# A float32 transformer block: the up projection of ten column quads as Strassen block products, and the down projection taken quad by quad with its sums added in DRAM

## Chip, cores and metric

The kernel runs on one core of one Trainium2 chip. Its time is device microseconds of one launch; the figure compared is the median of several launches. Engines are named as in the profile: PE (TensorE, matrix products), PEld (the weight loads of PE, which run beside its products), DVE (VectorE), ACT (ScalarE), POOL (GpSimd), SP (SyncE, which here only issues transfers).

## The reference

One block of a hybrid backbone: a token mixer of two scanned head groups and, behind it, a gated MLP. The change lies in the MLP, which works on 512 latent tokens (a grid of 8 rows by 64 columns), 2048 channels and 5504 hidden channels:

```python
h2 = rmsnorm(x, g_norm2) * (1 + sc2) + sh2
x = x + gt2 * conv_ffn(h2, rows, GRID_W, w_up, conv_w, conv_b, w_down)

def conv_ffn(h, rows, cols, w_up, conv_w, conv_b, w_down):
    u = jnp.einsum('btd,df->btf', h, w_up)
    u_gate, u_val = jnp.split(u, 2, axis=-1)
    g = lax.conv_general_dilated(u_gate.reshape(b, rows, cols, D_FF), conv_w[:, :, None, :],
                                 window_strides=(1, 1), padding='SAME',
                                 dimension_numbers=('NHWC', 'HWIO', 'NHWC'),
                                 feature_group_count=D_FF)
    g = g.reshape(b, t, D_FF) + conv_b
    return jnp.einsum('btf,fd->btd', jax.nn.silu(g) * u_val, w_down)
```

The convolution is depthwise, 3x3 and centred. A last RMS norm over channels gives the output. sh2, sc2 and gt2 are three of six slices of a modulation vector, one row times a 2048 x 12288 matrix. All inputs are float32.

## The kernel before

**Numbers and layout.** Activations lie channels by tokens: a tile is 128 channels (partitions) by 512 tokens. PE takes a reduced float32, so every operand is kept as a pair, the rounded value (h or hi) and the remainder (l or lo): `split` (L88 to L90) has ScalarE cast the value (L89) and VectorE subtract it (L90). `mm3` (L104) multiplies two such pairs with three matmuls, hi by hi, hi by lo and lo by hi, and all matmuls stand in the profile as L95. Likewise `mul` is L83 and `add` L86 wherever they are called.

**Weights.** They come in chunks of 512 KB, two row blocks of 128 by 512 columns. `load_split` (L162) asks SP for the chunk into one of the raw buffers of `wraw` (four), and splits it into one of two hi and one of two lo buffers (`whi`, `wlo`). `unit` (L197) is one product of 2048 channels by 512 output columns for all tokens: eight chunks, each with 4 column blocks x 2 row blocks x 3 matmuls of 512 columns, 192 matmuls into four PSUM accumulators. Pool psA has six of the eight PSUM banks and psB two.

**Order.** The code of `block_kernel` runs once, to lay out the program. A scheduler puts the instructions into each engine's queue in the order of the code, with those under `tc.high_priority()` moved ahead; where `pinned` is set, PE's order is exactly that of the code. A queue is worked in order, and each instruction waits for its inputs and for the tile that it reuses.

**Modulation as filler.** Four of the six slices of the modulation are summed on VectorE: `mod_chunk` (L259) loads a raw tile of `w_mod` and adds two rows of it, times a scalar, into a running sum (L272, L274). `mod_fillers` lists these pieces, and `load_split` takes some per chunk by a rate (`rate`, `credit`; the lists `UG_FILL` and `UV_FILL` in the MLP). The slice gt2 (region 5) is summed in the first quads of the MLP, since it is wanted only at the first residual.

**Stages in order.** Input projection with the scans woven in; gate projections `ga` (four units); output projection `wo` (four units), which ends with the residual into `x2`, kept in SBUF as 16 tiles, and the token norm. Then h2 (L1057 to L1066): for each of 16 row blocks VectorE scales x2 into `t`, a tile of a pool with two buffers, ScalarE casts it with the shift added, VectorE forms the remainder. Then the MLP by quads of four hidden row blocks (`QUADS`: ten of four and a last one of three):

- `up_gate` (L1092) is one unit on the gate columns. ScalarE copies each accumulator into a padded grid (L1099) and starts the convolution with one tap (L1106); VectorE adds eight taps (L1108), ScalarE applies silu. The first unit, `ug0`, starts while h2 is still being made: with `late` its first chunk takes all hi products of the two first row blocks ahead of those with a remainder (L183 to L189).
- `up_val` (L1113) is one unit on the value columns; VectorE multiplies each accumulator into the gated value, and the product is split into `gh` and `gl`.
- `down_block` (L1128) multiplies the products of a group of quads with 512 output columns of `w_down` and adds the four accumulators to x2 on VectorE, times gt2 (`residual`, L1004). `GROUPS` takes two quads at a time, and the last three together (11 row blocks); the four blocks of a group run between the gate unit and the value unit of the quad behind it.

**Tail.** Behind the last value unit come three blocks of the last group, with the squares for the last norm, then the fourth (`dl`) in two halves of 256 tokens. In the second half's matmuls, at places 10 and 18 of 44, PE takes the first half's norm (`token_rstd`) and VectorE, GpSimd and the output transfers take its scaling (`scaled`, L1170). The second half's own norm, scaling and outputs end the program.

## Time and profile before

| what | value |
|---|---|
| time, median of 3 launches (lowest, highest) | 2572.23 us (2571.21, 2572.74) |
| profiled execution: span on the chip | 2571.5 us |
| HBM read, written | 315.10 MB, 4.19 MB |
| granted PE clock, mean | 0.997 of full |
| busy time of the sixteen transfer engines, q1 (SP) | 36.8% of the span |

The busy line gives busy time per engine, its share of the span, and the number of instructions. The chain is the work that ended last, followed back from the end. In rows of groups, `out<-in` are the names of tiles with their numbers left out; behind the bar stand busy time and mean ns of one, then the idle time ahead of them and what ended it. Rows of a timeline give start, duration, engine, line, operation, tiles, shape and the number of like instructions in a row. Rows of windows give the stretch, its length, the busy time of PE, weight loads, VectorE, ScalarE and GpSimd with their counts, then granted clock, share of the transfer engines, and GB/s.

### The profile page before, as it was taken

The numbers are of one execution on the slowest core, as the hardware profiler recorded it, in microseconds if no ns is written. First come the engines' busy times: TensorE is split into PE (matmuls) and PEld (weight loads), VectorE is DVE, ScalarE is ACT, GpSimd is POOL, SyncE is SP. The second block draws the span as 40 slices with busy tenths as digits, with TensorE's granted clock in tenths as the row PEclk, the third lists the DMA queues.
The fourth block names the chain that finished last, engine by engine and source line by source line (L and its number), as shares of the span: only waits on it lengthen the run. The fifth ranks groups of instructions, "written<-read, shape, count | busy, mean of one in ns | idle before, by whom it ended". The sixth has DMA issues, their size and how long they took to land.

```text
span 2571.5 us, 31635 instructions
## 1 busy us (share of the span) xinstructions
PE 2532.5 (98%) x12944; PEld 2125.0 (83%) x12944; DVE 1399.4 (54%) x2071; ACT 789.2 (31%) x1177; POOL 25.1 (1%) x53
## 2 busy tenths in 40 slices
PE   6999999999999999999999999999999999999998
PEld 4887899888887888888888888888888888888887
DVE  6567755544446676549856335632663365336534
ACT  4225543322223242234323122312331233123332
POOL 0000000000000000000000000000000000000001
PEclk9999999999999999999999999999999999999999
DMA  9741111132335776325733332332232233322333
GB/s 384 265 166 34 34 42 49 59 96 86 130 126 191 250 270 236 129 81 166 259 99 98 98 99 94 95 98 99 99 97 93 97 99 99 99 95 88 101 94 107
DMA packets 96345, 321.35 MB, mean 125 GB/s; under 512 B 10884, under 2 KB 15304, under 8 KB 96200
## 3 DMA queue, kind: packets, MB, share of 16 engines
q1 hardware_dynamic: 95112, 318.29, 36.8%
q8 instruction: 101, 1.65, 0.3%
q10 hardware_dynamic: 1088, 1.05, 0.1%
q14 instruction: 44, 0.36, 0.0%
HBM read 315.10 MB, written 4.19 MB: 124 GB/s over the span
## 4 chain that ended last, share of the span: by engine, by line
PE 95%; DVE 3%; ACT 1%; issue 1%; DMA 0%; SPq 0%; DVEq 0%; ACTq 0%
PE a L95 19%; PE ug L95 18%; PE dn L95 17%; PE uv L95 17%; PE ga L95 7%; PE wo L95 7%; PE po L95 4%; PE ps_m L95 1%; PE sl L95 1%; PE dl L95 1%; DVE cv L1108 1%; PE cst L95 1%; PE s L95 1%; DVE sq_l L86 0%; PE gm L95 0%
## 5 line engine op out<-in xcount | busy, mean ns | idle before, releaser
L95 PE MATMUL uv<-h2h,hi_uv 128*128 128x512 f32 x688 | 267.7, 389 | 0.0
L95 PE MATMUL uv<-h2l,hi_uv 128*128 128x512 f32 x688 | 267.6, 389 | 0.0
L95 PE MATMUL uv<-h2h,lo_uv 128*128 128x512 f32 x688 | 267.6, 389 | 0.0
L95 PE MATMUL ug<-h2h,hi_ug 128*128 128x512 f32 x688 | 267.4, 390 | 0.0
L95 PE MATMUL ug<-h2h,lo_ug 128*128 128x512 f32 x688 | 266.7, 389 | 0.7 <-DVE lo_ug L90 0.7
L95 PE MATMUL ug<-h2l,hi_ug 128*128 128x512 f32 x688 | 266.6, 389 | 0.0
L95 PE MATMUL dn<-gh,hi_d 128*128 128x512 f32 x644 | 250.5, 389 | 0.0
L95 PE MATMUL dn<-gl,hi_d 128*128 128x512 f32 x644 | 250.5, 389 | 0.0
L95 PE MATMUL dn<-gh,lo_d 128*128 128x512 f32 x644 | 250.5, 389 | 0.0
L1108 DVE SCALAR_TENSOR_TENSOR cv<-pad,cwt,cv 128x512 f32<-128x512 f32 x344 | 237.5, 747 | 8.5 <-ACT cv L1106 7.2
L90 DVE TENSOR_TENSOR lo_ug<-raw_ug,hi_ug 128x1024 fp32r<-128x1024 f32 (+1 forms) x88 | 105.5, 1199 | 248.9 <-ACT hi_ug L89 248.9
L90 DVE TENSOR_TENSOR lo_uv<-raw_uv,hi_uv 128x1024 fp32r<-128x1024 f32 (+1 forms) x88 | 105.4, 1198 | 174.8 <-ACT hi_uv L89 174.4
L90 DVE TENSOR_TENSOR lo_d<-raw_d,hi_d 128x1024 fp32r<-128x1024 f32 x82 | 98.7, 1204 | 169.7 <-ACT hi_d L89 168.8
L274 DVE SCALAR_TENSOR_TENSOR sum_m<-raw_m,csil,sum_m 128x512 f32<-128x512 f32 x240 | 179.9, 750 | 19.5 <-DMA raw_m<-in_w_mod 13.9
L89 ACT CAST hi_ug<-raw_ug 128x1024 fp32r<-128x1024 f32 (+1 forms) x88 | 90.9, 1033 | 304.8 <-PE ug L95 220.9
L89 ACT CAST hi_d<-raw_d 128x1024 fp32r<-128x1024 f32 x82 | 85.1, 1037 | 278.7 <-PE dn L95 224.4
L89 ACT CAST hi_uv<-raw_uv 128x1024 fp32r<-128x1024 f32 (+1 forms) x88 | 90.8, 1032 | 257.0 <-PE uv L95 176.7
L95 PEld LDWEIGHTS ug<-h2h,lo_ug 128*128 128x128 f32 x688 | 129.2, 188 | 28.0 <-DVE lo_ug L90 1.3
L95 PEld LDWEIGHTS ug<-h2h,hi_ug 128*128 128x128 f32 x688 | 129.1, 188 | 27.6 <-issue 0.8
L95 PEld LDWEIGHTS uv<-h2h,hi_uv 128*128 128x128 f32 x688 | 129.2, 188 | 26.8
L95 PEld LDWEIGHTS uv<-h2h,lo_uv 128*128 128x128 f32 x688 | 129.2, 188 | 26.7
L95 PEld LDWEIGHTS uv<-h2l,hi_uv 128*128 128x128 f32 x688 | 129.2, 188 | 26.7
(307 smaller groups left out, 4934.0 us busy)
## 6 DMA issues: line engine op xcount, KB each, us to landing
raw_m<-in_w_mod SPq DMA_DIRECT2D x192, 512.0 KB, 5.0
raw_ug<-in_w_up SPq DMA_DIRECT2D x80, 512.0 KB, 3.3
raw_uv<-in_w_up SPq DMA_DIRECT2D x80, 512.0 KB, 3.4
raw_d<-in_w_down SPq DMA_DIRECT2D x79, 512.0 KB, 3.4
raw_h<-in_w_heads SPq DMA_DIRECT2D x64, 512.0 KB, 3.3
raw_ga<-in_w_gates SPq DMA_DIRECT2D x32, 512.0 KB, 4.2
raw_wo<-in_w_out SPq DMA_DIRECT2D x32, 512.0 KB, 3.3
xl<-in_xT SPq DMA_DIRECT2D x16, 256.0 KB, 5.1
```

Source lines behind the costliest of these rows:

```text
L89: S.copy(hi, x)
L90: return V.tensor_tensor(out=lo, in0=x, in1=hi.bitcast(F32), op=ALU.subtract).ins
L95: ins = PE.matmul(*args, **kw)
L274: V.scalar_tensor_tensor(out=parts[0], in0=x, scalar=ck, in1=parts[0], op0=ALU.mult, op1=ALU.add)
L1108: V.scalar_tensor_tensor(out=t3, in0=src, scalar=w, in1=t3, op0=ALU.mult, op1=ALU.add)
```

## The change

**Up projection.** A unit is a product of a 2 x 2 block matrix (per chunk two row blocks of channels; two halves of 256 hidden columns) with another (the two row blocks; two halves of 256 tokens). For the ten quads of four it becomes Strassen's seven products, in the form that shares sums. `load_sums` takes the place of `load_split`: the raw tile has 7 x 256 columns, four quarters from DRAM and three sums on VectorE (`add` three times, one of them over a quarter no longer needed), and the split covers all 1792 columns. The tokens' operands are four halves `bq` (one of them overwritten later by a sum, `token_last`) and three sums `bt`, hi and lo each, made once by `token_sums`. `seven` issues 7 products x 2 column blocks x 3 matmuls of 256 columns for each of eight chunks, into seven PSUM tiles out of a pool of eight banks (`psM`). `four` folds the seven sums into the four quarters of the output through two tiles u and v. In a gate unit `put` writes a quarter into the padded grid; in a value unit it multiplies it into the gated value and, once both token halves are there, splits the products.

**Order of quads.** The quad of three comes first and stays in plain form, and the token sums are made behind its gate unit in the code. h2's first step writes over x2 in place of a tile `t`, after x2 has been stored to DRAM (`x2d`).

**Down projection.** It runs quad by quad between the next quad's gate and value unit. `down_sums` has ScalarE copy each accumulator into one of three staging tiles (`stp`), and GpSimd's queue adds it to DRAM with an accumulating transfer: for the first nine quads to `dacc`, unscaled, for the next to `x2d`, times gt2. `fold`, behind the down stage of the ninth quad (index `FOLD` = 8), reads `dacc` back, scales it, and adds it to `x2d`. At the end x2 is read back into SBUF. The modulation pieces are spread over these down stages at 0.7 a chunk in place of the two lists.

**Tail.** The last group has four row blocks in place of eleven, so the first half's norm and scaling stand at places 4 and 8 of 16. The weights of `w_up` are cut accordingly.

```diff
-QUADS = [4] * 10 + [3]
-GROUPS = [[0, 1], [2, 3], [4, 5], [6, 7], [8, 9, 10]]
+QUADS = [3] + [4] * 10
+NQ = len(QUADS)
+FOLD = NQ - 3
...
+    def fill():
         credit[0] += rate[0]
         while credit[0] >= 1:
             credit[0] -= 1
             if fillers:
                 fillers.pop(0)()
...
+    def load_sums(src, name):
+        x = wts[0].tile([P, 7, HW], F32, name=f"raw_{name}", tag="raw")
+        hi = wts[1].tile([P, 7, HW], F32R, name=f"hi_{name}", tag="hi")
+        lo = wts[2].tile([P, 7, HW], F32R, name=f"lo_{name}", tag="lo")
+        nc.sync.dma_start(x[:, 0:4, :], src.rearrange("p a (b c) -> p (a b) c", c=HW))
+        with tc.high_priority():
+            add(x[:, 4:6, :], x[:, 0:4:3, :], x[:, 1:2, :].to_broadcast([P, 2, HW]))
+            add(x[:, 6, :], x[:, 5, :], x[:, 0, :])
+            add(x[:, 1, :], x[:, 2, :], x[:, 6, :])
+            split(hi, lo, x)
+        fill()
         return hi, lo
...
+    x2d = [dram.tile([P, T], F32, name=f"x2d{k}", tag=f"x{k}") for k in range(KT)]
+    dacc = [dram.tile([P, T], F32, name=f"dacc{k}", tag=f"d{k}") for k in range(KT)]
...
+                nc.gpsimd.dma_start(x2d[4 * n + i], x2[4 * n + i])
...
+    wts[:] = [pool(ctx, "mraw", 3, waits="tile"), pool(ctx, "mhi", 2, waits="tile"), pool(ctx, "mlo", 2, waits="tile")]
+    bp = pool(ctx, "bp", waits="tile")
+    fp = pool(ctx, "fp", waits="tile")
+    stp = pool(ctx, "stp", 3, waits="tile")
+    mod_raw.append(wts[0])
+    rate[0] = 0
...
+    bq = [[operand(j, part, "q", f"bq{part}{j}", (P, 4, HW)) for j in range(KP)] for part in "hl"]
+    bt = [[operand(j, part, "t", f"bt{part}{j}", (P, 3, HW)) for j in range(KP)] for part in "hl"]
+    h2 = [[flat(b[k // 2][:, 2 * (k % 2) : 2 * (k % 2) + 2, :]) for k in range(KT)] for b in bq]
...
-            t = gp.tile([P, T], F32, name=f"h2_{k}", tag="h2")
             sk, bk = modc[4][:, k : k + 1], modc[3][:, k : k + 1]
-            h2[0].append(acttile(k, "h", f"h2h{k}"))
-            h2[1].append(acttile(k, "l", f"h2l{k}"))
-            V.scalar_tensor_tensor(out=t, in0=x2[k], scalar=sk, in1=r2, op0=ALU.mult, op1=ALU.mult)
-            S.activation(h2[0][k], t, AF.Identity, bias=bk)
-            V.scalar_tensor_tensor(out=h2[1][k], in0=t, scalar=bk, in1=h2[0][k].bitcast(F32), op0=ALU.add,
+            V.scalar_tensor_tensor(out=x2[k], in0=x2[k], scalar=sk, in1=r2, op0=ALU.mult, op1=ALU.mult)
+            S.activation(h2[0][k], x2[k], AF.Identity, bias=bk)
+            V.scalar_tensor_tensor(out=h2[1][k], in0=x2[k], scalar=bk, in1=h2[0][k].bitcast(F32), op0=ALU.add,
                                    op1=ALU.subtract)
-    st_3.close()
-    st_h.close()
-    fp = pool(ctx, "fp")
-    tp = pool(ctx, "tp", 4)
-    mod_raw.append(pool(ctx, "mraw4", 3))
+    st_p.close()
+    banks8.append(pool(ctx, "psM", 8, PSUM, waits="tile"))
...
+    def token_sums(j):
+        k0, k1 = 2 * j, 2 * j + 1
+        for k in (k0, k1):
+            S.activation(x2[k], x2[k], AF.Identity, bias=modc[3][:, k : k + 1])
+        sub(half(k0, 0), half(k0, 1), half(k0, 0))
+        sub(half(k0, 1), half(k0, 1), half(k1, 1))
+        sub(half(k1, 1), half(k1, 1), half(k0, 0))
+        sub(half(k1, 0), half(k1, 1), half(k1, 0))
+        split(flat(bt[0][j][:, 0:2, :]), flat(bt[1][j][:, 0:2, :]), x2[k0])
+        split(bt[0][j][:, 2, :], bt[1][j][:, 2, :], half(k1, 1))
+    def token_last(j):
+        split(bq[0][j][:, 1, :], bq[1][j][:, 1, :], half(2 * j + 1, 0))
...
-    UG_FILL = [(0, 0, 0, 0, 1, 1, 1, 1), (1, 2, 2, 3, 3, 3, 2, 1), (2, 2, 3, 3, 3, 3, 1, 0)]
-    UV_FILL = (0, 0, 0, 0, 0, 0, 1, 2)
...
+    PRODUCTS = ((0, bq, 0), (2, bq, 2), (6, bt, 2), (4, bt, 1), (5, bt, 0), (1, bq, 3), (3, bq, 1))
+    def seven(src, name):
+        ps = [acc(f"{name}_{n}", (P, 2, HW)) for n in range(7)]
+        for kp in range(KP):
+            wh, wl = load_sums(src[kp], f"{name}_{kp}")
+            for o, (s, b, c) in zip(ps, PRODUCTS):
+                for m in range(2):
+                    ms = slice(P * m, P * m + P)
+                    mm3(o[:, m, :], wh[:, s, ms], wl[:, s, ms], b[0][kp][:, c, :], b[1][kp][:, c, :],
+                        kp == 0 and m == 0, kp == KP - 1, skip_group_check=True)
+        return ps
+    def four(ps, name, put):
+        p1, p2, p6, p7, p5, p3, p4 = ps
+        u, v = ytile(9, f"u_{name}", (P, 2, HW)), ytile(11, f"v_{name}", (P, 2, HW))
+        with tc.high_priority():
+            S.copy(u, p1)
+            put(0, 0, u, p2, ALU.add)
+            sub(u, u, p6)
+            sub(v, p7, u)
+            put(1, 1, v, p5, ALU.add)
+            sub(u, u, p5)
+            put(0, 1, u, p3, ALU.add)
+            put(1, 0, v, p4, ALU.subtract)
+    def first_f(q):
+        return 4 * q - 1 if q else 0
...
+        if q == 0:
+            accs = unit(a["w_up3"][0], "ug0", *h2, n=3, late=True)
+            with tc.high_priority():
+                for i, ps in enumerate(accs):
+                    S.copy(pads[:, i, 1 : ROWS + 1, 1 : GW + 1], ps.rearrange("p (r c) -> p r c", c=GW))
+        else:
+            def put(mh, th, x, ps, op):
+                V.tensor_tensor(out=pads[:, 2 * mh : 2 * mh + 2, 1 + 4 * th : 5 + 4 * th, 1 : GW + 1],
+                                in0=x.rearrange("p m (r c) -> p m r c", c=GW),
+                                in1=ps.rearrange("p m (r c) -> p m r c", c=GW), op=op)
+            four(seven(a["w_up4"][2 * q - 2], f"ug{q}"), f"ug{q}", put)
...
+        def product(i):
+            gh, gl = (ytile(2 * i + n, f"g{p}{first_f(q) + i}", dtype=F32R) for n, p in enumerate("hl"))
+            split(gh, gl, convs[i])
+            gs[first_f(q) + i] = (gh, gl)
+        if q == 0:
+            accs = unit(a["w_up3"][1], "uv0", *h2, n=3)
             with tc.high_priority():
-                mul(convs[i], convs[i], ps)
-                gh = fp.tile([P, T], F32R, name=f"gh{f}", tag=f"gh{f % 8 if q < 10 else 8 + i}")
-                gl = fp.tile([P, T], F32R, name=f"gl{f}", tag=f"gl{f % 8 if q < 10 else 8 + i}")
-                split(gh, gl, convs[i])
-            gs[f] = (gh, gl)
-    def fspan(qs):
-        return [f for q in qs for f in range(4 * q, 4 * q + QUADS[q])]
-    def down_block(fs, blk):
-        accs = [acc(f"dn{fs[0]}_{blk}_{i}") for i in range(4)]
+                for i, ps in enumerate(accs):
+                    mul(convs[i], convs[i], ps)
+                    product(i)
+        else:
+            def put(mh, th, x, ps, op):
+                t = ytile(13, f"t{q}_{mh}{th}", (P, 2, HW))
+                V.tensor_tensor(out=t, in0=x, in1=ps, op=op)
+                for i in range(2):
+                    c = convs[2 * mh + i][:, HW * th : HW * th + HW]
+                    mul(c, c, t[:, i, :])
+                if mh != th:
+                    for i in range(2):
+                        product(2 * mh + i)
+            four(seven(a["w_up4"][2 * q - 1], f"uv{q}"), f"uv{q}", put)
...
+    def down_sums(q):
+        for blk in range(4):
+            accs = down_block(q, blk)
+            with tc.high_priority():
+                for i in range(4):
+                    k = 4 * blk + i
+                    t = stp.tile([P, T], F32, name=f"st{q}_{k}", tag="st")
+                    S.activation(t, accs[i], AF.Copy, scale=modc[5][:, k : k + 1] if q > FOLD else 1.0)
+                    if q == 0:
+                        nc.gpsimd.dma_start(dacc[k], t)
+                    else:
+                        nc.gpsimd.dma_start(x2d[k] if q > FOLD else dacc[k], t, accum_op=ALU.add)
+    def fold():
+        assert not fillers
+        for k in range(KT):
+            t = stp.tile([P, T], F32, name=f"fold{k}", tag="st")
+            nc.gpsimd.dma_start(t, dacc[k])
+            S.activation(t, t, AF.Copy, scale=modc[5][:, k : k + 1])
+            nc.gpsimd.dma_start(x2d[k], t, accum_op=ALU.add)
+    for q in range(NQ):
+        up_gate(q)
+        if q == 0:
+            for j in range(KP):
+                token_sums(j)
+        if q:
+            rate[0] = 0.7 if q < FOLD + 1 else 0
+            down_sums(q - 1)
+            rate[0] = 0
+        if q - 1 == FOLD:
+            fold()
+        up_val(q, convolve(q))
+        if q == 0:
+            with tc.high_priority():
+                for j in range(KP):
+                    token_last(j)
+    tc.keep_in_program_order(S.preload_act_table_set("natural_log_exp_and_others"))
+    q = NQ - 1
+    fs = list(range(first_f(q), NF))
+    xf = [operand(j, "h", "q", f"xf{j}", (P, 2, T), F32) for j in range(KP)]
+    x2 = [xf[k // 2][:, k % 2, :] for k in range(KT)]
+    for k in range(KT):
+        nc.gpsimd.dma_start(x2[k], x2d[k])
...
-            if hf and at in (10, 18):
+            if hf and at in (4, 8):
...
-    r["w_up4"] = np.stack([blocks(w_up[:, FF * s + 512 * q : FF * s + 512 * q + 512], 512)
+    r["w_up4"] = np.stack([blocks(w_up[:, FF * s + 384 + 512 * q : FF * s + 896 + 512 * q], 512)
                            for q in range(10) for s in range(2)])
-    r["w_up3"] = np.stack([blocks(w_up[:, FF * s + 5120 : FF * s + 5504], 384) for s in range(2)])
+    r["w_up3"] = np.stack([blocks(w_up[:, FF * s : FF * s + 384], 384) for s in range(2)])
```

128 lines of the change are left out of this document (69 added, 59 removed).

## The prediction

> **What bounds the kernel now.** I read the page's busy line and chain first, then who TensorE (PE) waited for, then single matmuls, then what one matmul unit of the up projection leaves the other engines.
>
> ```profile
> PE 2532.5 (98%) x12944; PEld 2125.0 (83%) x12944; DVE 1399.4 (54%) x2071; ACT 789.2 (31%) x1177; POOL 25.1 (1%) x53
> ...
> PE 95%; DVE 3%; ACT 1%; issue 1%; DMA 0%; SPq 0%; DVEq 0%; ACTq 0%
> ```
> ```profile
> PE ss_l L95 <- DVE sq_l L86: 19.6, 1, 19.6
> ```
> The chain is PE from end to end, and outside the start (19.6 us) PE hardly waits. So every matmul removed is worth its spacing, and every wait put into PE's queue costs its length. Spacing is read from start to start, since a matmul's own length (0.39 us) overlaps the next:
>
> ```profile
> 1500.08 0.39 PE L95 MATMUL ug<-h2h,hi_ug 128*128 128x512 f32 x1
> 1500.31 0.39 PE L95 MATMUL ug<-h2l,hi_ug 128*128 128x512 f32 x1
> ```
> ```profile
> 2535.87 0.28 PE L95 MATMUL dl<-gh,dll 128*128 128x256 f32 x1
> 2535.99 0.28 PE L95 MATMUL dl<-gh,dlh 128*128 128x256 f32 x1
> ```
> ```profile
> 1146.70:1190.20 43.50, 43.48 (x192) 36.02 (x193) 41.09 (x52) 20.79 (x28) 2.42 (x4) 1.00 0.45 147
> 1500.00:1543.50 43.50, 43.50 (x194) 36.03 (x193) 14.15 (x16) 12.80 (x16) 0.00 (x0) 1.00 0.30 97
> ```
> A unit of 192 matmuls of 512 columns takes 43.5 us: 0.2266 each, 5.44 us per weight chunk. A matmul of 256 columns starts every 0.120 us: per column 6% dearer. In the second window (columns: PE, weight loads, DVE, ACT, POOL) VectorE is busy 14 of 43.5 us and ScalarE 13. That slack is what the change spends.
>
> **Matmuls.** Ten quads have two units each of Strassen form: 8 chunks x 7 products x 2 halves x 3 = 336 matmuls of 256 columns, 336 x 0.120 = 40.3 us against 43.5. That is 3.2 us for each of 20 units, **-64 us**; not an eighth, because the halves are narrow. The last group shrinks from 11 row blocks to 4, so 168 fewer matmuls run at half width: 84 x 0.2266 - 168 x 0.120 = -1 us. The Trainium skill, "TensorE: Matmul & The Clock Gate", section "Back-to-back issue gap", puts the spacing at columns/2.4 + 2.5 ns, which would make the gain 95 us. This trace shows 227 and 120 ns where that gives 216 and 109, so the measurement decides.
>
> **Weight preparation.** Prices, by form:
>
> ```profile
> L1108 DVE SCALAR_TENSOR_TENSOR cv<-pad,cwt,cv 128x512 f32<-128x512 f32 x344 | 237.5, 747 | 8.5 <-ACT cv L1106 7.2
> L90 DVE TENSOR_TENSOR lo_ug<-raw_ug,hi_ug 128x1024 fp32r<-128x1024 f32 x80 | 97.9, 1223 | 227.4 <-ACT hi_ug L89 227.4
> L90 DVE TENSOR_TENSOR gl<-cv,gh 128x512 fp32r<-128x512 f32 x43 | 29.5, 687 | 0.1
> L90 DVE TENSOR_TENSOR lo_ug<-raw_ug,hi_ug 128x768 fp32r<-128x768 f32 x8 | 7.7, 958 | 21.5 <-ACT hi_ug L89 21.5
> ```
> ```profile
> L89 ACT CAST hi_ug<-raw_ug 128x1024 fp32r<-128x1024 f32 x80 | 84.2, 1053 | 281.7 <-PE ug L95 202.1 <-PE uv L95 39.5 <-issue 30.4
> L89 ACT CAST gh<-cv 128x512 fp32r<-128x512 f32 x43 | 26.6, 619 | 33.9 <-DVE cv L83 32.9
> L1099 ACT COPY pad<-ug 128x512 f32<-128x512 f32 x43 | 25.3, 588 | 6.1 <-PE ug L95 6.1
> L89 ACT CAST hi_ug<-raw_ug 128x768 fp32r<-128x768 f32 x8 | 6.7, 838 | 23.1 <-PE ug L95 18.7 <-PE uv L95 4.3
> ```
> ```profile
> 1195.28 4.72 DVE L1108 SCALAR_TENSOR_TENSOR cv<-pad,cwt,cv 128x512 f32<-128x512 f32 x7
> ```
> ```profile
> 1222.93 3.90 DVE L274 SCALAR_TENSOR_TENSOR sum_m<-raw_m,csil,sum_m 128x512 f32<-128x512 f32 x5
> ```
> ```profile
> 1500.20 0.69 DVE L90 TENSOR_TENSOR gl<-cv,gh 128x512 fp32r<-128x512 f32 x1
> 1500.81 1.22 DVE L90 TENSOR_TENSOR lo_ug<-raw_ug,hi_ug 128x1024 fp32r<-128x1024 f32 x1
> ```
> ```profile
> 2549.53 1.08 DVE L83 TENSOR_TENSOR o<-x,rb_rmsf 128x256 f32<-128x256 f32 x3 [1.97 <-ACT r3s L1173]
> ```
> In a row VectorE starts a tap every 0.66 us (4.72 for 7), a dependent sum every 0.78, a 512-wide add every 0.61, a 256-wide one every 0.34. A chunk now carries 1792 columns instead of 1024. By the slopes between the 768 and 1024 rows the cast takes 1.70 us and the remainder 2.02, with three additions before them (0.7 + 0.45 + 0.34): about 3.4 us of VectorE per 5.04 us of PE (42 x 0.120). Both operand buffers are double, so cast and remainder of chunk k+2 run after chunk k's last matmul: 0.2 + 1.70 + 2.02 = 3.9 of 5.04 us. Inside a unit that is hidden with 1.1 us to spare: **0**. Where VectorE has other work in its queue it isn't.
>
> **From a value unit to the next gate unit.** The seven sums are folded there (copy, four outputs, eight half products, four splits), in the same queue as the new unit's chunks. In the changed program's VectorE queue 5.0 us of work end with the remainder of chunk 1 and 9.8 us with that of chunk 2. Counting from the value unit's end: remainder 1 ends at 4.0, then 7.9 us of other work, remainder 2 ends at 14.1. PE has 84 matmuls (10.1 us) and 14 more that need only the cast; it gets through those at 13.7, waits, and ends chunk 2 at 17.4 instead of 15.1. So 2.3 us, nine times: **+21** (bounds: 0.5 each where the spacings shorten, 5 each where every hand-over costs more).
>
> **Down stage.** 43.5 us of PE for 16 blocks. VectorE has 32 taps, eight remainders and the first additions, 5.1 to 5.9 us per 5.44 us chunk by the queue. It keeps some 2 us ahead until it reaches a modulation sum whose raw tile shares the three raw buffers; the tile is asked for when the chunk before frees its buffer and lands 4.6 us later:
>
> ```profile
> raw_ug<-in_w_up SPq DMA_DIRECT2D x72, 512.0 KB, 3.2
> raw_m<-in_w_mod SPq DMA_DIRECT2D x21, 512.0 KB, 4.6
> ```
> ```profile
> out<-o SPq DMA_DIRECT2D x12, 256.0 KB, 2.7
> ```
> That is 2.9 us of VectorE standing still, which eats the lead and leaves about 1 us for PE to wait, in eight quads: **+8** (0 to 3 each). ScalarE's 16 copies (0.59) take the place of VectorE's residuals and fit. Each waits for one of three staging tiles, freed when the accumulating transfer three before it ends. A block's sums end 6 x 0.2266 = 1.36 us apart, so its first copy starts 4.1 us before the block's end and lasts 0.6; the fourth must start 4.8 us after that end, or the next cast (5.44 after it) is late: harmless up to a latency of 4.1 - 0.6 + 4.8 = 8.3 us. No row shows such a transfer. Below: the 2.7 us of a plain store. Above: fetch, load and store in turn behind traffic, 2.7 + 5.0 + 2.7 = 10.4, using raw_m's 5.0 below. I take 5, nearer the store: 0. The Trainium skill, "DMA: Bandwidth & Descriptors", section "Anatomy of one DMA", gives 2.0 us plus size over 436 GB/s for GpSimd's queue, an estimate of 2.6 us here; no run yet shows it.
>
> ```profile
> raw_m<-in_w_mod SPq DMA_DIRECT2D x192, 512.0 KB, 5.0
> ...
> raw_dl<-in_w_down SPq DMA_DIRECT2D x11, 256.0 KB, 2.9
> ```
> The fold sends 16 tiles through the same three buffers in one value unit: (2.9 + 0.7 + 5 + 0.5) / 3 = 3.0 us each, 49 us against 40, with ScalarE's casts queued behind its waits: **+8** (0 to 35, the latter with 10.4).
>
> **First unit.** Now VectorE alternates:
>
> ```profile
> 1145.16 1.41 DVE L1063 SCALAR_TENSOR_TENSOR h<-x,mod,rb_rms 128x512 f32<-128x512 f32 x2 [2.42 <-PE rb_rms L95]
> 1146.70 1.41 DVE L1065 SCALAR_TENSOR_TENSOR h2l<-h,mod,h2h 128x512 fp32r<-128x512 f32 x2
> ...
> 1153.88 1.22 DVE L90 TENSOR_TENSOR lo_ug<-raw_ug,hi_ug 128x1024 fp32r<-128x1024 f32 x1
> ...
> 1142.00:1144.00 2.00, 2.00 (x12) 2.00 (x11) 0.60 (x4) 0.15 (x1) 0.00 (x0) 0.50 0.67 236
> ```
> The two-deep h buffer paced it; with x2 overwritten in place nothing does, and in the changed queue all the rest of the 32 operations (31 x 0.66), ten half sums and four splits stand before the remainder of chunk 2: 27.4 us after remainder 1, that is at about 1174. Chunk 0 gets its second operand row at about 1151, chunk 1 ends 4.1 us after it is done, near 1156; PE stands 18 us, then has six chunks of 18 x 0.2266 = 4.1 us and ends near 1200 instead of 1179: **+21** (10 to 25). Half clock after a lull is in the last row (0.50); I put 1.7 us of it in the 21. [...]
>
> **Rest.** Token sums' tail, first Strassen quad and its three-block down stage, whose queue leaves no lead: +3. After the last value unit the down matmuls need that unit's own products: fold chain, cast 0.62 and remainder 0.69 end some 5 us after it, with clock +6. The tail's second half now has 16 x 3 x 0.120 = 5.8 us of matmuls instead of 15.8 to hide the first half's norm and outputs: its last residual, 0.49 us at 2558.48 with PE free, now queues behind the output products (4.7 us, 2549.53 to 2554.27), +4.
>
> ```profile
> 2552.62 1.65 DVE L1179 SCALAR_TENSOR_TENSOR o<-x,cols,rb_rmsf 128x256 f32<-128x256 f32 x4
> ```
> ```profile
> 2558.48 0.49 DVE x L1004
> ```
> In the gate stage four modulation sums move ahead of a remainder on VectorE, and the two convolution loads ahead of weight loads on SP: +1 (0 to 3). The 16 early stores of x2 and its reload lie beside PE: 0; bare, the first reload would cost 2.9.
>
> Sum: -64 - 1 + 21 + 8 + 8 + 21 + 3 + 6 + 4 + 1 = **+7** on the span of 2571.5, and 0.7 us lies between it and the median of 2572.2: **2579**.
>
> **Rivals.** (1) *Faster: PE doesn't wait at the hand-overs.* VectorE isn't full (9.8 of 15 us there), only its order hurts; if remainder 2 comes within 12 us of the value unit's end and the down stage keeps its lead, 21 + 8 + 3 go: 2547. It decides from 1 us of wait per hand-over down. By the page's spacing the sum would end at 2548, near this rival's time; with both widths measured otherwise it gets 0.01, inside this rival's chance. (2) *The staging tiles bind.* From 8.3 us latency each further microsecond holds ScalarE, and with it the next cast, four times in each of ten quads: 40 us per microsecond, at 10.4 us +84, 2663. For it: additions double a transfer's DRAM traffic; against: DMA share is 0.30 in the steady window. (3) *No gain at all:* narrow matmuls pace at the weight load, 0.188 us as the page has it: 336 x 0.188 = 63.2, 2965. Against: 0.120 above, with a load for each.
>
> **Chances.** Forecast 0.48 (own range 2560 to 2605), (1) 0.36, (2) 0.14, (3) 0.02. Runs of this kernel can tell 0.2% (5.1 us) from no change. Faster: nearly all of (1) and 0.05 of the forecast, 0.40; same 0.10; slower 0.50. Range 2540 to 2630, from (1) less its 7 us of fold to half of (2).
>
> **What would show it.** Strassen matmuls 0.120 us apart; a PE wait of 15 us or more on the remainder of chunk 2 in the first gate unit; in later gate units one of 1 to 4 us on that same remainder; no ScalarE wait on a staging tile over 1 us outside the fold; some 5 us at the last down stage. A narrow spacing above 0.125, or waits in the middle of units, would break the sum.

## The result, and the profile after

| kernel | time, us: median (lowest to highest) | span of the profiled execution |
|---|---|---|
| before | 2572.48 (2571.21 to 2573.83), 4 runs | 2571.5 |
| changed | 2650.47 (2647.36 to 2654.82), 4 runs | 2653.1 |

The ratio is 1.0305, with a 95% interval of 1.029 to 1.0319: 78 us slower, where 7 us were forecast. The profiled execution of the changed kernel is the longest of its four, 4 us above the median. The page of the changed kernel, its span, busy line, transfer queues and chain:

```profile
span 2653.1 us, 38849 instructions
PE 2513.1 (95%) x15740; PEld 2230.2 (84%) x15740; DVE 1805.1 (68%) x2720; ACT 993.5 (37%) x1370; POOL 200.3 (8%) x274
...
q1 hardware_dynamic: 94680, 318.29, 35.9%
q0 software_dynamic: 28160, 58.73, 12.1%
...
PE 67%; DVE 14%; DMA 10%; issue 7%; POOL 1%; ACT 1%; SPq 0%; DVEq 0%; POOLq 0%; ACTq 0%
```

PE no longer carries the chain alone: 10% of it are transfers and 14% VectorE. Whom PE waited for, from the waits of PE (in all, times, longest):

```profile
PE uv L97 <- DVE lo_uv L92: 32.7, 16, 4.6
PE dn L97 <- DVE lo_d L92: 19.7, 13, 3.2
...
PE ug L97 <- DVE x L1109: 17.8, 1, 17.8
PE ug L97 <- ACT hi_ug L91: 11.8, 11, 2.6
PE uv L97 <- ACT hi_uv L91: 6.6, 4, 3.4
...
PE ug L97 <- DVE lo_ug L92: 4.9, 13, 1.6
```

The largest is the value unit's remainder, of which the prediction had nothing; 8.9 of its 32.7 us lie in the unit with the fold. One row for each kind of stage shows the same from the windows (columns as before: PE, weight loads, VectorE, ScalarE, GpSimd, granted clock, share of the transfer engines): the first unit, a gate unit, a down stage, a value unit behind a down stage, the value unit with the fold, the last value unit.

```profile
1146.30:1199.50 53.20, 35.38 (x148) 28.84 (x147) 45.86 (x88) 35.76 (x58) 0.00 (x0) 0.81 0.19 60
1354.20:1396.90 42.70, 41.37 (x338) 40.57 (x337) 35.26 (x50) 15.47 (x13) 0.00 (x0) 1.00 0.36 116
1397.00:1443.60 46.60, 44.60 (x201) 35.94 (x201) 40.17 (x59) 22.20 (x32) 10.48 (x12) 1.00 0.81 197
1443.60:1494.70 51.10, 45.04 (x337) 44.60 (x336) 30.08 (x35) 15.07 (x12) 3.54 (x4) 0.90 0.41 104
2390.70:2450.90 60.20, 46.02 (x337) 44.39 (x335) 28.51 (x33) 24.04 (x25) 23.73 (x33) 0.91 0.90 208
2542.70:2590.00 47.30, 40.76 (x337) 40.31 (x335) 31.97 (x38) 15.60 (x13) 10.48 (x18) 0.99 0.73 216
```

The value unit at 1443.6 has the same 336 matmuls as the gate unit ahead of it and takes 51.1 us in place of the 40.3 of its matmuls, while VectorE works only 30 of them. Its first 13 us, as the chain of that window goes:

```profile
1443.91 2.02 DVE lo_uv L92
1445.92 0.03 DVE raw_uv L88
1445.95 8.15 DMA raw_uv<-in_w_up
1454.10 0.03 issue
...
1454.25 0.55 issue
1454.80 2.03 DVE lo_uv L92
1456.83 0.04 issue
1456.87 5.28 PE uv L97 x23
```

Remainder 0 ends at 1445.92 and sets a raw tile free. The load into it, chunk 3's, takes 8.15 us. Remainder 1, which PE needs, comes only behind the addition to chunk 3. VectorE's queue in this unit has them in this order (from the built program, buffer numbers shortened):

```
L88 raw_uv2_2 128x512
L88 raw_uv2_2 128x256
L92 lo_uv2_0
L88 raw_uv2_2 128x256
L88 raw_uv2_3 128x512
L92 lo_uv2_1
```

So a load that starts only after remainder 0 stands in front of remainder 1. The additions to chunk 2 stand ahead of remainder 0 likewise, and they do in every Strassen value unit. Those to chunk 3 stand ahead of remainder 1 in quads 2, 3 and 6 only. While the load ran, four accumulating transfers of the last block of the down stage were under way, issued from 1443.61 to 1448.52. The issues, median from issue to landing in the last column:

```profile
raw_ug<-in_w_up SPq DMA_DIRECT2D x80, 512.0 KB, 3.5
raw_uv<-in_w_up SPq DMA_DIRECT2D x80, 512.0 KB, 5.3
dacc<-st POOLq DMA_DIRECT2D x144, 256.0 KB, 5.5
```

Loads of the same size land in 3.5 us in gate units and in 5.3 in value units, which follow the down stages.

**Where the 81.6 us of span came from.** For every stage I take the distance from its first matmul to the first one of the next stage, less its matmuls at 0.120 or 0.2266 us. What is left is wait, and time lost at half clock behind a wait.

| term of the sum | predicted | measured |
|---|---|---|
| matmuls of the units and of the tail | -65 | -65 |
| first unit | +21 | +20.5 |
| value to gate unit, nine times | +21 | +23 |
| inside value units of quads 1 to 8, behind a down stage | 0 | +36.4 |
| down stages (with the three-block one and the last) | +8 and +3 | +38.8 |
| fold (value unit 9, and 4.6 in the gate unit behind it) | +8 | +24.5 |
| last value unit to the down stage | +6 | +7.0 |
| tail | +4 | +0.8 |
| start of the MLP; waits of before's quads 1 and 2 that went | +1 | -4.8 |

The 36.4 us of the value units are of three kinds. PE waited 11.0 us for remainder 0, in six of the eight units, and 11.2 us for a later one, of which 4.1, 4.6 and 2.1 are for remainder 1 in quads 2, 3 and 6. Most of the rest is half clock: these units ran 26 us at a granted clock of 0.50, which costs 13. The unit of quad 5, in which PE found both remainders done, takes 40.6 us:

```profile
1862.40:1903.00 40.60, 40.52 (x337) 40.31 (x336) 28.02 (x32) 14.58 (x10) 2.79 (x4) 1.00 0.47 131
```

### The profile page after: what moved, and what is told of

Its sections match the earlier page's. It is cut to its first block, busy times and chain, and to the rows that moved or that the text cites. A ratio compares the mean times of both kernels' runs of the same rounds, so it can differ in the third digit from the quotient of the medians.

```text
span 2653.1 us, 38849 instructions
## 1 busy us (share of the span) xinstructions
PE 2513.1 (95%) x15740; PEld 2230.2 (84%) x15740; DVE 1805.1 (68%) x2720; ACT 993.5 (37%) x1370; POOL 200.3 (8%) x274
## 3 DMA queue, kind: packets, MB, share of 16 engines
q0 software_dynamic: 28160, 58.73, 12.1%
## 4 chain that ended last, share of the span: by engine, by line
PE 67%; DVE 14%; DMA 10%; issue 7%; POOL 1%; ACT 1%; SPq 0%; DVEq 0%; POOLq 0%; ACTq 0%
PE a L97 18%; PE uv L97 12%; PE ug L97 10%; PE ga L97 7%; PE wo L97 7%; PE dn L97 4%; DMA raw_m<-in_w_mod 4%; PE po L97 3%; DMA raw_uv<-in_w_up 3%; DVE cv L1208 2%; DVE lo_ug L92 2%; DVE lo_d L92 2%; DVE raw_ug L88 1%; PE sl L97 1%; PE ps_m L97 1%
## 5 line engine op out<-in xcount | busy, mean ns | idle before, releaser
L97 PE MATMUL dn<-gh,lo_d 128*128 128x512 f32 x672 | 266.0, 396 | 19.8 <-DVE lo_d L92 19.7
L1208 DVE SCALAR_TENSOR_TENSOR cv<-pads,cwt,cv 128x512 f32<-128x512 f32 x344 | 240.1, 749 | 2.2 <-ACT cv L1206 1.6
L97 PE MATMUL uv<-bqh,lo_uv 128*128 128x256 f32 (+1 forms) x688 | 205.1, 299 | 32.8 <-DVE lo_uv L92 32.7
L92 DVE TENSOR_TENSOR lo_uv<-raw_uv,hi_uv 128x1792 fp32r<-128x1792 f32 (+1 forms) x88 | 169.2, 1926 | 96.6 <-ACT hi_uv L91 96.5
L97 PE MATMUL ug<-bqh,hi_ug 128*128 128x256 f32 (+1 forms) x688 | 201.1, 296 | 31.5 <-DVE x L1109 17.8
L92 DVE TENSOR_TENSOR lo_ug<-raw_ug,hi_ug 128x1792 fp32r<-128x1792 f32 (+1 forms) x88 | 168.7, 1925 | 74.2 <-ACT hi_ug L91 74.1
L97 PE MATMUL uv<-bqh,hi_uv 128*128 128x256 f32 (+1 forms) x688 | 203.2, 295 | 6.6 <-ACT hi_uv L91 6.6
L97 PE MATMUL uv<-bql,hi_uv 128*128 128x256 f32 (+1 forms) x688 | 202.7, 295 | 0.0
L97 PE MATMUL ug<-bqh,lo_ug 128*128 128x256 f32 (+1 forms) x688 | 197.8, 298 | 5.0 <-DVE lo_ug L92 4.9
L97 PE MATMUL ug<-bql,hi_ug 128*128 128x256 f32 (+1 forms) x688 | 197.9, 291 | 0.0
L97 PEld LDWEIGHTS dn<-gh,lo_d 128*128 128x128 f32 x672 | 127.7, 190 | 52.9 <-DVE lo_d L92 26.5
L97 PE MATMUL a<-hi_h,hTh 128*128 128x256 f32 x512 | 150.5, 294 | 0.5 <-ACT e L391 0.5
```

What stands on the lines that cost most here:

```text
L92: return V.tensor_tensor(out=lo, in0=x, in1=hi.bitcast(F32), op=ALU.subtract).ins
L97: ins = PE.matmul(*args, **kw)
L1208: V.scalar_tensor_tensor(out=t3, in0=src, scalar=w, in1=t3, op0=ALU.mult, op1=ALU.add)
```

## The experiments

Waits in us by stage, read as above, in one profiled execution of each kernel; "value 9" is the unit with the fold, "down" are all eleven down stages.

| kernel | time | first unit | gate units | value 1 to 8 | value 9 | value 10 | down |
|---|---|---|---|---|---|---|---|
| changed | 2650.5 | 20.5 | 28.3 | 36.4 | 19.9 | 7.0 | 38.8 |
| e1_store | 2614.3 | 20.5 | 30.6 | 18.9 | 20.2 | 5.2 | 15.1 |
| e2_no_transfer | 2598.7 | 20.5 | 28.8 | 8.1 | 19.6 | 5.2 | 11.3 |
| e3_no_modulation | 2621.9 | 20.1 | 29.4 | 19.7 | 23.2 | 9.0 | 18.1 |
| e4_plain_products | 2627.9 | 20.0 | 1.1 | 0.1 | 23.1 | 0.0 | 14.2 |
| e5_banks | 2656.6 | 20.1 | 32.0 | 35.0 | 21.5 | 9.3 | 36.1 |
| e6_banks_order | 2654.4 | 12.5 | 33.4 | 36.9 | 23.1 | 8.1 | 35.8 |
| e7_fold_gpsimd | 2636.6 | 20.5 | 27.2 | 39.6 | 5.5 | 6.9 | 32.1 |
| e8_four_raw | 2595.3 | 20.0 | 10.8 | 0.1 | 24.5 | 5.2 | 29.1 |
| e9_three_raw | 2600.4 | 20.0 | 7.0 | 2.1 | 22.9 | 5.2 | 39.4 |
| e10_repairs | 2555.7 | 9.7 | 2.7 | 1.0 | 0.0 | 5.2 | 32.1 |
| e11_early_gate | 2534.3 | 8.7 | 2.2 | 0.0 | 0.0 | 5.2 | 10.0 |
| e12_order_only | 2611.4 | 20.2 | 23.5 | 5.9 | 23.4 | 5.2 | 28.8 |
| e13_split_only | 2671.2 | 20.5 | 39.4 | 38.0 | 22.7 | 10.4 | 37.0 |
| e14_norm_copied | 2643.3 | 1.7 | 35.0 | 35.8 | 22.3 | 7.5 | 36.4 |
| e15_free_bank | 2530.2 | 0.4 | 5.8 | 0.0 | 0.0 | 5.2 | 9.7 |

The kernel before had medians of 2573 to 2575 us on the same chips. e11 and e15 have four runs, the other experiments one. On VectorE, ScalarE and PE e5 has the instructions of the changed kernel in the same order, so its row shows how far a row moves by itself: up to 3.7 us in a column and 6 in the time.

### What the accumulating transfers do: e1 and e2

e1 stores in place of adding; e2 takes the same line out altogether, with its `else`:

```diff
-                        nc.gpsimd.dma_start(x2d[k] if q > FOLD else dacc[k], t, accum_op=ALU.add)
+                        nc.gpsimd.dma_start(x2d[k] if q > FOLD else dacc[k], t)
```

> The down sums of quads 1 to 9 are stored over DRAM's tiles in place of added to them (so their additions are left out). Theory T1 (transfers): the accumulating transfers fill the transfer engines in bursts, weight and modulation tiles land late, VectorE takes them in order and PE waits behind it; a plain store costs the engines less time, so the 33 us of waits in the value units of quads 2 to 8 halve and the down stages lose a third of theirs: about 25 us, 2628. Theory T2 (VectorE's own work and order): the order is the same, so 2645 to 2652. Theory T3 (staging tiles hold ScalarE and its casts): the store lands sooner, ScalarE's 54 us of waits on staging tiles go, some 15 us, while VectorE's 93 us of waits on value weights stay.

> Only quad 0's sums go to DRAM; the transfers of quads 1 to 9 are left out (ScalarE still copies to the staging tiles). T1: the value units' 33 us fall to some 8, the down stages' 30 to some 15, about 45 us in all: 2608; VectorE's waits on value weights fall from 93 us to under 40. T2: within 8 us of the changed kernel. T3: as T1 in time, but VectorE's waits on value weights stay near 93 us.

Instructions and their order on VectorE, ScalarE and PE are those of the changed kernel in e1, and in e2 but for a few around the fold. The time fell by 36 and 52 us, more than T1 asked for. VectorE's waits for value weights and modulation tiles, e1 first, then e2:

```profile
DVE raw_uv L88 <- DMA raw_uv<-in_w_up: 59.0, 37, 4.6
...
DVE sum_m L298 <- DMA raw_m<-in_w_mod: 11.5, 11, 2.5
```
```profile
DVE raw_uv L88 <- DMA raw_uv<-in_w_up: 51.9, 30, 4.1
...
DVE sum_m L298 <- DMA raw_m<-in_w_mod: 5.6, 8, 1.8
```

In the changed kernel these two rows, and ScalarE's for the staging tiles, read:

```profile
DVE raw_uv L88 <- DMA raw_uv<-in_w_up: 93.2, 39, 7.9
...
ACT st L1259 <- DMA dacc<-st: 54.3, 26, 5.1
...
DVE sum_m L298 <- DMA raw_m<-in_w_mod: 26.8, 14, 4.8
```

The waits on loads shrink, though those on value weights stay at 52 us where T1 asked for under 40; what the value units lose by them falls from 36.4 to 8.1. The loads themselves are no longer late: in e1 those of the value units land in 4.1 us, and in e2 in about what a gate unit's take:

```profile
raw_uv<-in_w_up SPq DMA_DIRECT2D x80, 512.0 KB, 3.6
```

The page of e1 shows why a plain store is cheaper:

```profile
q0 software_dynamic: 18944, 58.73, 6.8%
```

The queue moves the same 58.73 MB in 18944 packets in place of 28160, and takes 6.8% of 16 engines' span in place of 12.1%. T1 stands and T2 falls: with VectorE's work untouched 52 us go.

### What the modulation pieces do: e3

```diff
-    mod_fillers((5,))
+    V.memset(modc[5], 0.1)
```

> The sums of the last modulation slice are left out (a constant stands for it): 32 loads of 512 KB and 64 VectorE instructions fewer in the down stages of quads 0 to 7. T1: the loads no longer meet the accumulating transfers there; the down stages lose 20 of their 35 us and the value units 10 of 36: 2623. T2: VectorE has 42 us less work in these stages, 1.2 us a chunk: the down stages' waits go, 30 us, and the value units start with VectorE ahead: 2610. If the fills don't matter, 2645 or more.

29 us. The down stages lose 20 of their 39 us and the value units 17 of 36, as T1 had it; T2's 2610 was not reached, and the waits of 18 us that stay in the down stages are without a filler. So transfers and fillers both add to the same delay.

### What Strassen's form pays for itself: e4

```diff
-            four(seven(a["w_up4"][2 * q - 1], f"uv{q}"), f"uv{q}", put)
+            accs = unit(a["w_up4"][2 * q - 1], f"uv{q}", *h2)
...
-                token_sums(j)
```

> All units as plain products of 192 wide matmuls (43.5 us each), down projection quad by quad through DRAM as in the changed kernel; no token sums. 64 us of matmul gain are gone. T1: gate units lose their 28 us of waits, value units nearly all of their 36 + 20 (VectorE has no additions and 0.8 us less remainder a chunk), down stages keep half of 35: 2620 to 2635, the first unit still with its 20 us. T2: all waits but the first unit's go: 2600. If the down projection through DRAM carries the loss by itself, 2680 or more.

With 64 us more of matmuls this kernel is 23 us faster than the changed one. But for the fold's, gate and value units have no waits, though the transfers and pieces are all there, and the down stages 14 us in place of 39. Left over are 54 us above the kernel before, of which 20 are the first unit and 23 the fold. The late loads, then, cost PE little where VectorE has no additions to make and a shorter remainder.

### The order of the additions, the ring and the pieces: e8, e9, e12, e13

e8 holds the four quarters in raw tiles of their own, four deep, the sums in two tiles, and makes the split in two parts; to make room, one running sum of the modulation moves into the tile of constants. e9 is e8 with three raw tiles.

```diff
-        x = wts[0].tile([P, 7, HW], F32, name=f"raw_{name}", tag="raw")
+        x = wts[0].tile([P, 4, HW], F32, name=f"raw_{name}", tag="raw")
+        s = wts[3].tile([P, 3, HW], F32, name=f"sum_{name}", tag="sum")
...
-            split(hi, lo, x)
+            split(hi[:, 0:4, :], lo[:, 0:4, :], x)
+            split(hi[:, 4:7, :], lo[:, 4:7, :], s)
```

> Raw weight tiles are cut from 7 to 4 quarters and there are four of them in place of three; the sums have two tiles of their own (a split is two casts and two subtractions). If late loads are what costs, through the short ring of raw tiles: a load may be 5 us later without a wait; the value units of quads 2 to 8 fall from 33 us of waits to under 10, the down stages from 30 to 15: 2612. If the ring is deep enough and VectorE's amount of work decides, two more instructions a chunk make it no faster: 2650 to 2665.

> The kernel of e8 with three raw tiles of four quarters in place of four, all else alike. Theory R (the depth of the raw ring absorbs late loads): the waits return, 25 to 35 us in the value units of quads 2 to 8, 2630 to 2650. Theory P (it was the split in two, with the sums in tiles of their own): as e8, 2595 to 2605.

e8 gained 55 us: its value units of quads 1 to 8 are at 40.3 us, all matmul. But e9 has nearly the same value units with three tiles, so the depth is not what they needed; in the down stages it may be worth some 10 us (29.1 against 39.4, one run each). Theory R falls. Of what e8 and e9 share two things matter here: with two sum tiles the additions of chunk 3 cannot be put ahead of remainder 1, and the pieces are smaller (a raw tile is then free after the first of two remainders). e12 and e13 part order and size, on the changed kernel. e12 keeps a list `los` of the remainders and puts a chunk's additions behind the last but one:

```diff
-            add(x[:, 4:6, :], x[:, 0:4:3, :], x[:, 1:2, :].to_broadcast([P, 2, HW]))
...
-            split(hi, lo, x)
+            with tc.issue_after(los[-2]):
+                add(x[:, 4:6, :], x[:, 0:4:3, :], x[:, 1:2, :].to_broadcast([P, 2, HW]))
...
+            los.append(split(hi, lo, x))
```

e13 makes the split in two:

```diff
-            split(hi, lo, x)
+            split(hi[:, 0:4, :], lo[:, 0:4, :], x[:, 0:4, :])
+            split(hi[:, 4:7, :], lo[:, 4:7, :], x[:, 4:7, :])
```

> The changed kernel with one order: a chunk's three additions come behind the remainder of the chunk two before it (in the changed kernel the wide addition of chunk 3 stands ahead of remainder 1, so that this waits for a load that only remainder 0 lets start). Theory O: that inversion is what costs; the value units of quads 2 to 8 fall from 33 us of waits to under 10: 2620 to 2630. Theory H (size of the pieces): they keep more than 20 us, 2640 to 2655.

> The changed kernel with the split of a chunk as two casts and two subtractions (four quarters, three sums) out of the same raw tile of seven quarters. Theory H: PE can start on the quarters 1.5 us earlier and the first remainder no longer stands for 2.0 us; gate units lose their 2.4 us each, value units most of 33: 2600 to 2620. Theory O: the additions of chunk 3 still stand ahead of remainder 1's end, the value units keep 20 us or more; the gate units may gain: 2630 to 2650.

The order alone takes the value units from 36.4 to 5.9 us, with every transfer and piece in place, and the kernel from 2650 to 2611. The edge holds for all twenty Strassen units and towards the remainders of the down weights too: the down stages lose 10 us and the gate units 5, while the unit with the fold takes 3.5 more. The split alone made the kernel 21 us slower, which neither theory gave; in its built order an addition for another chunk stands between the two parts of each remainder, whose cost wasn't measured by itself. Two things were needed for the loss in value units, loads made late by the transfers and an order that puts such a load in front of what PE waits for; taking either away ends most of it (8.1 us left in e2, 5.9 in e12). The waits of e12 also dispose of T3:

```profile
PE uv L97 <- DVE lo_uv L92: 11.2, 11, 1.6
...
ACT st L1262 <- DMA dacc<-st: 52.9, 29, 4.8
```

ScalarE waits for staging tiles as long as before (52.9 against 54.3 us), and PE does not mind. Which of e8's edits helped the gate units (28.3 to 10.8, of which 8.9 are left in the one behind the fold) was not parted.

### The first unit: e5, e6, e14

e5 adds three lines; e6 also emits h2's rows 8 to 15 and the token sums behind remainders of the unit:

```diff
     banks8.append(pool(ctx, "psM", 8, PSUM, waits="tile"))
+    for n in range(3):
+        acc(f"skip_{n}")
```
```diff
+            for _ in unit_steps(a["w_up3"][0], "ug0", *h2, accs, True):
+                for at in (2, 3):
+                    if len(los) == first + at + 1 and len(done) == at - 2:
+                        done.append(at)
+                        with tc.issue_after(los[-1]):
+                            tokens(range(4 * at, 4 * at + 4), r2s)
...
+                with tc.issue_after(late_los[min(j + 3, KP - 1)]):
+                    token_sums(j)
```

> Three accumulators are passed over ahead of the first gate unit, so that it takes other PSUM banks than the one in which the token norm lies. Theory B (bank): the first unit's second matmul waits 18 us for the last of 16 operations that read the norm out of the bank that it is to write; without it the unit ends 18 us earlier: 2632. Theory Q (queue, as predicted): VectorE's queue has 31 operations and the first token sums ahead of the remainder of chunk 2, so PE only stands later, at chunk 2, until about 1171 us, and the unit ends within 3 us of where it did: 2648.

> The same banks, and the order on VectorE: the second half of h2's rows behind the remainders of chunks 2 and 3, the token sums behind those of chunks 3 to 7 (the norm is copied to SBUF for the late rows). B and Q together: the first unit lasts 34 to 36 us in place of 53, 2632, if e5 alone gained nothing. If B alone is right this gains no more than e5.

e5 told nothing: a tile that is never written takes no bank, and the accumulators stayed where they were. In e6 PE waited 10.1 us for the norm's copy, which stood late in ScalarE's queue, so the 8 us that it gained are no verdict on either theory. In the built program the norm and the first unit's second accumulator both lie in bank 7. e14 makes the copy first and leaves the order of the code alone:

```diff
+        S.copy(r2s, r2)
...
-            V.scalar_tensor_tensor(out=x2[k], in0=x2[k], scalar=sk, in1=r2, op0=ALU.mult, op1=ALU.mult)
+            V.scalar_tensor_tensor(out=x2[k], in0=x2[k], scalar=sk, in1=r2s, op0=ALU.mult, op1=ALU.mult)
```

> The changed kernel with the token norm copied to SBUF ahead of its 16 readers, so that its PSUM bank is free 1 us later; VectorE's order stays. Theory B: PE goes on from its second matmul and the first unit ends some 16 us earlier, 2634. Theory Q (as predicted): PE gets through chunks 0 and 1 and then stands at chunk 2 until its remainder, at about 1171 us; the unit ends within 4 us of where it did, 2647 to 2652.

PE's timeline at the first unit, changed kernel, then e14:

```profile
1146.33 0.47 PE L97 MATMUL ug<-bqh,hi_ug 128*128 128x512 f32 x1
1164.63 0.77 PE L97 MATMUL ug<-bqh,hi_ug 128*128 128x512 f32 x1 [17.82 <-DVE x L1109]
```
```profile
1146.83 0.96 PE L97 MATMUL ug<-bqh,hi_ug 128*128 128x512 f32 x3
```

PE's second matmul waited for L1109, the last of 16 operations that read the norm out of the bank that it was to write. With the bank free the first unit takes 34.4 us in place of 53.2. Theory B holds for the wait that PE had. The whole kernel gained only 7 us, in one run: the first Strassen gate unit gave back 4, since the token sums now come late for it, and the rest lies in single units further on, within what e5's row moves by itself. Theory Q's stall did not follow, because the built order changed with it. In the changed kernel remainder 2 starts at 1171.97, behind all rows of h2. In e14 it stands behind 7 of the 16 scalings and 5 of the 16 remainders of h2:

```profile
1153.51 0.75 DVE L1113 SCALAR_TENSOR_TENSOR bql<-x,mod,bqh 128x512 fp32r<-128x512 f32 x1
1154.17 0.95 DVE L92 TENSOR_TENSOR lo_ug<-raw_ug,hi_ug 128x768 fp32r<-128x768 f32 x1
```

So Theory Q is not refuted. Had the bank been free and the order kept, PE would have stood until remainder 2 was done at 1172.9, and six chunks of 4.1 us from there end at about 1197 (an estimate), 2 to 3 us before the 1199.5 measured. No run frees the bank with that order kept.

### The fold, and the repairs together: e7, e10, e11, e15

```diff
-            S.activation(t, t, AF.Copy, scale=modc[5][:, k : k + 1])
+            G.tensor_scalar(out=t, in0=t, scalar1=modc[5][:, k : k + 1], scalar2=None, op0=ALU.mult)
```

> The fold's 16 multiplications run on GpSimd, which waits for nothing else, in place of ScalarE. Theory S: ScalarE stands 39 us on the fold's loads with weight casts behind it; without that the value unit of quad 9 falls from 60.3 to 42 to 44 us and the gate unit behind it from 47.3 to 43: 2628 to 2630. Theory T1 (the 32 extra transfers delay the weight loads): the value unit stays above 50 us, 2640 or more.

The value unit of quad 9 fell from 60.3 to 45.9 us with all 32 transfers in place, some 2 us above Theory S's 42 to 44, and the time, 2636.6, lies between the two theories. The greater part, then, was ScalarE, which in the changed kernel waits

```profile
ACT fold L1271 <- DMA fold<-dacc: 39.1, 15, 6.5
```

with weight casts behind it. The gate unit behind it hardly gained (46.4 us from 47.3).

> The four raw tiles of e8, the fold on GpSimd of e7, and for the first unit the order of e6 with the norm copied to SBUF ahead of everything that reads it, so that its bank is free at once. If the three repairs are independent: e8 less some 20 us of fold and 17 us of the first unit, 2558. If the first unit's wait is not the norm's bank, it keeps 10 of its 20 us: 2566.

> As e10, but the last modulation slice is summed ahead of the MLP (2.3 pieces a chunk in the gate and output projections in place of 1.5), so that all ten quads add their sums, scaled, to the stream in DRAM and there is no fold and no filler in the down stages. If VectorE and the transfers have the room that the profile of before shows there (VectorE 26 of 44 us): the fold's 33 us, most of the down stages' 26 us of waits and 17 us of the first unit go from e8's 2595: 2520 to 2535. Rival: the gate and output stages become longer by 10 to 30 us, since 2.3 pieces ask for 1.4 MB a chunk: 2540 to 2560.

e10 came out at 2555.7: with e8's preparation and the multiplications on GpSimd the fold costs nothing (40.3 us), but the down stages keep 32 us. In e11 there are no pieces in them, and nine of its ten stages ahead of the last value unit have 0.4 us of waits together, with the accumulating transfers all there (the three-block one has 6.4). e10 is e8 with e7's line and e6's order, the norm's copy first; e11 adds this:

```diff
-    mod_fillers((2, 3, 4))
+    mod_fillers((2, 3, 4, 5))
...
-                    S.activation(t, accs[i], AF.Copy, scale=modc[5][:, k : k + 1] if q > FOLD else 1.0)
+                    S.activation(t, accs[i], AF.Copy, scale=modc[5][:, k : k + 1])
+                    nc.gpsimd.dma_start(x2d[k], t, accum_op=ALU.add)
```

e11 took 2534.29 us (2533.43 to 2535.48), a ratio of 0.9845 to the kernel before with an interval of 0.9828 to 0.9861. The pieces cost little where they went: the MLP starts at 1149.7, and at 1144.8 to 1148.2 in the kernels without them. e11's first unit keeps 8.7 us, of which PE waits 6.2 for a remainder of h2 that the order by hand puts late. e15 is e11 with e14's copy in place of the order by hand.

> As e11, with the norm's copy of e14 in place of the order by hand. If the bank was all: first unit 34 us in place of 41, the rest as e11: 2525 to 2529. If the token sums come late for it, the first Strassen unit gives 4 us back, as in e14 (44.7 against 40.8): 2529 to 2533.

```profile
span 2527.8 us, 39241 instructions
...
PE 2477.2 (98%) x15740; PEld 2212.4 (88%) x15740; DVE 1820.1 (72%) x2880; ACT 1017.9 (40%) x1515; POOL 182.2 (7%) x242
```
```profile
ACT st L1260 <- DMA x2d<-st: 59.8, 49, 4.3
```

2530.18 us (2529.53 to 2531.90), ratio 0.9832 (0.9816 to 0.9849), the fastest of all: the first unit is whole and the unit behind it pays 3.9 us, as the expectation's second case had it. ScalarE waits 59.8 us for staging tiles here, more than in the changed kernel, at no cost.

## Why the prediction was wrong

**The step that failed** is in the weight preparation: "Inside a unit that is hidden with 1.1 us to spare: **0**." It followed the two operand buffers alone: cast and remainder fit between a chunk's last matmul and the next but one. The prediction's next sentence excepts other work in VectorE's queue, but only the hand-over to the gate unit was priced for that. The sum left out the raw tile's loop, in which a remainder sets the tile free, the load follows, and the additions to that load stand in VectorE's queue ahead of a later remainder. Gate units behind a value unit, with loads of 3.5 us, lose 2.3 to 3.2 us each (the one behind the fold 7), nearly all at the hand-over; in the value unit above a load of 8.15 us stood in front of remainder 1, and PE waited 4.1 us for it and then ran at half clock. Measured: 36.4 us where 0 was taken (e12: 5.9 with the order mended).

**The transfers** were asked only who waits for their staging tiles. The cost was right: 5 us were taken, 5.5 measured (the longest 9.8), the bound was 8.3, and e12 and e15 show ScalarE's waits to be free. The sign was not: no wait over 1 us was to be seen on a staging tile, and there were 26 waits, 54.3 us in all and up to 5.1 each. But "DMA share is 0.30 in the steady window" was read as room, where the bursts count: the share is 0.81 in the down stage above, and a load that met a burst took 8.15 us in place of 3.5. The rival of the staging tiles named a time near the measured one, and is refuted as a mechanism. On their price, the Trainium skill, "DMA: Bandwidth & Descriptors", section "Anatomy of one DMA", gives figures that make an estimate of 2.6 us for a transfer of this size through GpSimd's queue; the plain stores of x2 through it took 3.0 here, and the accumulating ones 5.5.

**Down stages**, +8 and +3, measured 38.8. The mechanism was named (VectorE stands on a raw tile of the modulation) and mis-sized: 2.9 us of standing a stage were taken, from a landing time of 4.6 without accumulating transfers. In the seven stages in which VectorE waited for modulation tiles it stood 3.9 us a stage for them, 4.8 at the longest, and 2.9 more for the value weights of the next unit, which the sum did not have. Without pieces and with the finer preparation it is 0.4 for nine stages (e11).

**Fold**, +8, measured 24.5. The chain through three staging tiles was right and its pace too fast: 3.0 us a tile were taken, and ScalarE's scalings came 3.7 us apart (from 2399.34 to 2455.17, 15 steps). From the first load's issue to the last addition's landing it was 65.8 us where 49 were worked out; a load took 4.5 us (median) in place of the 2.9 in that sum. With ScalarE's casts between them PE stopped at several places, and its clock fell: the window of that unit has 0.91. What a wait of a few microseconds does to the clock is seen behind the one that ended at 1456.87:

```profile
1458.00:1464.00 6.00, 6.00 (x33) 6.00 (x33) 3.09 (x4) 0.00 (x0) 0.00 (x0) 0.58 0.47 167
```

Shorter ones did it too: behind the waits of 1.95 us that ended at 1445.98 and of 2.14 us that ended at 2000.85 the granted clock was 0.50 for 3.4 us, while behind one of 1.72 us that ended at 2130.79 it stayed at 1.00.

**First unit**, +21, measured 20.5, and yet by another wait: PE stood for the norm's PSUM bank, not for remainder 2 (e14). The queue was as read, with remainder 2 at 1171.97 against "about 1174", but it never came to bear, and e14's build moved remainder 2 ahead as soon as the bank was free. That the number fits is luck: the bank, which the prediction did not have, was free at about the time at which the queue would have let PE go on. The row of the kernel before that was read as half clock "after a lull" shows the half clock alone: PE was busy for 3.73 of the 4 us up to 1140.

**Right as argued:** the spacing of 0.120 us and the -65 us of matmuls; the last value unit, 7 against 6. The nine hand-overs came out in size, 23 us against 21, but not by the wait of 1 to 4 us on the remainder of chunk 2 that was to show it: at the gate unit of 1354.2 PE waited 0.9 us for the cast of that chunk, which stood in ScalarE's queue behind a cast for the gated product, and 0.2 for its remainder:

```profile
1366.06 0.38 PE L97 MATMUL ug<-bqh,hi_ug 128*128 128x256 f32 x1 [0.92 <-ACT hi_ug L91]
1368.18 0.39 PE L97 MATMUL ug<-bqh,lo_ug 128*128 128x256 f32 x1 [0.20 <-DVE lo_ug L92]
```
```profile
1363.79 0.62 ACT L91 CAST gh<-cv 128x512 fp32r<-128x512 f32 x1 [7.72 <-DVE cv L85]
1364.32 3.28 ACT L91 CAST hi_ug<-raw_ug 128x1792 fp32r<-128x1792 f32 x2
```

The tail cost 0.8 in place of 4, and 4 us of waits that the kernel before had in its second and third gate unit went away uncounted. The range's upper end of 2630 is said to be "half of (2)", but half of that rival's 84 us on 2579 is 2621. The formula that the prediction takes from the Trainium skill, "TensorE: Matmul & The Clock Gate", section "Back-to-back issue gap", is given there for an isolated matmul, so the 95 us are no forecast for this stream.

## What to carry to other kernels

When work is put into an engine's slack, follow each buffer's whole loop through the queue, load included, and price the load at the time that it takes while the new transfers run, not at its quiet median. A load in front of a result in an in-order queue ties the result to the load: the order in twenty units, changed by one edge per chunk, was worth 39 us here at no change of the work. A tile that is read until late holds its PSUM bank for whoever comes next, and the order that a scheduler builds around that may change when it is freed.

## What was not expected of the hardware

An accumulating transfer to DRAM through GpSimd's queue moves in packets half as long as a plain transfer's through the same queue: by the trace's packets 2048 bytes at 178 ns (median) against 4096 bytes at 159 ns. So it holds the transfer engines 2.2 times as long for the same bytes. A load beside four of them at the end of a block took 8.15 us, and the median of the value units' loads, 5.3 us with these transfers, is 3.6 without them (e2).
